# Unused bytes ahead of the activations' buffers: their place relative to the weights' buffers becomes 1216 bytes on by 4096, or 192 by 256

## The chip, the cores and the metric

The kernel runs on one core of a Trainium2 chip. The metric is the device time of one execution in microseconds (us); lower is better. Three executions of the kernel before gave 930.80, 931.08 and 932.78 us, a median of 931.08.

## What is computed

Two layers over 256 tokens of 1024 features, in float32. A layer normalizes its input by the root mean square, makes from it the inputs of four kinds of attention (stick breaking, gated linear, gated delta rule, dilated) and a gate for each, adds up the gated branches and projects them, and then runs an MLP of width 4096 with a squared ReLU:

```
h = rms_norm(x, g_mix)
sb, gla, dn, dil inputs, gate_logits = split(h @ w_in)
o_n = branch n (stick breaking, gated linear attention, delta rule, dilated)
merged = sum over n of sigmoid(gate_logits[n]) * (o_n @ w_branch[n])
x = x + merged @ w_out
h = rms_norm(x, g_mlp)
x = x + square(relu(h @ w_mlp_in)) @ w_mlp_out
```

## The kernel before

**The stream of weights.** All weights are cut into 140 units of 1 MB, 70 to a layer, and each unit into two halves of 512 KB (`raw`, one DMA each). `split_part` (L246 to L248) parts every half into a high part `whi` (ScalarE, L247) and a low part `wlo` (VectorE, L248), both float32r. `split_upto` keeps this three halves ahead of the unit in use (`LEAD`). There are 6 buffers for `raw` and 5 each for `whi` and `wlo`, all of 4096 bytes in a partition.

**The products.** An activation is parted in the same way: `ah` and `al` hold the normalized input, `uh` and `ul` what lies between the two products of the MLP, `oh` and `ol` the output of a branch, `mh0` to `mh3` and `ml0` to `ml3` the merged branches. A float32 product is three float32r products (high by high, high by low, low by high), each with 128 rows, 128 stationary columns and 256 moving columns. A half of a unit is 24 of these. They are all issued by the helper `mm` (L199), and I call them the big products. The small products are those of the branches.

- Feature-major units (`unit_F`: dn_q, dn_k, dn_v, gla_q, sb_q, sb_k, the gates, the first product of the MLP): the weights are stationary, `ah` and `al` move. The output is a bank `bg`.
- Token-major units (`unit_T`: seven in a layer, inT in the list of units): `ah` and `al` are stationary, the weights move.
- The branch products (`unit_br`) move `oh` and `ol`. The projection `wo` and the second product of the MLP are `units_out`: for each half, eight outputs of three products each, with `mh`, `ml` or `uh`, `ul` moving, into banks `fa` and `fb`.

**The order.** It is written out by hand. Per layer: the units of `SEQ` with the four branches, `wo` (4 units), the first product of the MLP (16 units), the second (16 units). The small work of the branches runs in four chains (generators) that go forward by one step at each half of a unit; a table of pauses tells how many halves lie between a step and the one that reads it. All engines work in program order. Early in each mixing part POOL scales x (L369), ScalarE and VectorE rewrite `ah` and `al` from that (`flip`), and TensorE waits for it.

**Where the buffers lie.** Tiles are placed one after the other, in the order in which they are first asked for in their pool: `cons`, `wp` (raw, whi, wlo), `acts` (ah, al), `sm` (small ones), and after these the tiles of the layer's mixing part or of its MLP. Ahead of all lies a scratch region for descriptors of 16384 bytes. With the sizes of the tiles this gives the first byte of each buffer in its partition. What is left of it when multiples of 4096 are taken away:

| buffers | before | distance to the weights by 4096 | by 256 |
|---|---|---|---|
| raw, whi, wlo (all of them) | 2784 | 0 | 0 |
| ah, al | 2784 | 0 | 0 |
| uh, ul | 4000 | 1216 | 192 |
| oh, ol, mh, ml and most of the mixing part | 2240 or 192 (some 1216, 3264) | 3552 or 1504 | 224 |

Inside the buffers the big products step by 512 or 1024 bytes, so that the distance by 256 is the same for every one of a kind.

```
def mm(o, l, r, start=True, stop=True):
    PE.matmul(o, l, r, start=start, stop=stop, skip_group_check=True)
```

In `mm` the second argument is the stationary operand, the third the moving one.

Of the kernel before, what the change touches and what calls it, by code (L numbers as in the profile page):

```python
# [73 lines left out]
# columns of the packed parameters of a layer  # L74
P_GMIX, P_GMLP, P_CONV, P_DTB, P_ALOG, P_GLAB = 0, 8, 16, 40, 44, 48
P_GLAG, P_DNG, P_DILQ, P_DILK, P_LR2, NPAR = 49, 113, 177, 241, 305, 433
# columns of the constants
C_ID, C_NEGU, C_NEG1, C_UT, C_GT, C_STR, C_SBN, C_DIL = 0, 128, 256, 384, 512, 640, 768, 896
C_COS, C_SIN, C_SEL, C_S32, C_I32, C_H4, C_AB, NCON = 1280, 1312, 1344, 1346, 1378, 1410, 1414, 1422
LV = (1, 2, 4, 8, 16, 32, 64)  # L80

# [37 lines left out]
def lay_out(inp):  # L119
    a = {k: np.asarray(v) for k, v in inp.items()}  # L120
    w_in, w_br, w_out, w_mi, w_mo = (a[k] for k in ("w_in", "w_branch", "w_out", "w_mlp_in", "w_mlp_out"))
    W = np.zeros((len(UNITS), 128, 2048), np.float32)

    def kcols(w, c0, n=256):
        """[p][kt][column]"""
        return w[:, c0:c0 + n].reshape(8, 128, n).transpose(1, 0, 2).reshape(128, 8 * n)

    def fcols(w, c0):
        """[p][half of the columns][kt][column]"""
        return w[:, c0:c0 + 256].reshape(8, 128, 2, 128).transpose(1, 2, 0, 3).reshape(128, 2048)  # L130

    def krows(w, r0, halves=1):
        """[p][half of the columns][kt][column]"""
        n = 1024 // halves
        return w[r0:r0 + 256].reshape(2, 128, halves, n).transpose(1, 2, 0, 3).reshape(128, 2048)

    for n, (l, kind, arg) in enumerate(UNITS):
        if kind == "inF":
            W[n] = fcols(w_in[l], OFF[arg])
        elif kind == "inT":  # L140
            W[n] = kcols(w_in[l], OFF[arg])
        elif kind == "mini":
            m = np.zeros((1024, 32), np.float32)
            m[:, 0:8] = w_in[l][:, 2320:2328]
            m[:, 8:24] = w_in[l][:, 1280:1296]
            W[n][:, :256] = kcols(m, 0, 32)
        elif kind == "gate":
            W[n] = fcols(w_in[l], OFF["gates"] + arg[0] * 1024 + arg[1] * 256)
        elif kind == "br":
            W[n] = krows(w_br[l, arg], 0, 2)  # L150
        elif kind == "wo":
            W[n] = krows(w_out[l], arg * 256)
        elif kind == "mi":
            W[n] = fcols(w_mi[l], arg * 256)
        else:
            W[n] = krows(w_mo[l], arg * 256)
    P = np.zeros((NL, 128, NPAR), np.float32)
    for l in range(NL):
        P[l][:, P_GMIX:P_GMIX + 8] = a["norm_mix_g"][l].reshape(8, 128).T
        P[l][:, P_GMLP:P_GMLP + 8] = a["norm_mlp_g"][l].reshape(8, 128).T  # L160
        P[l][:, P_CONV:P_CONV + 24] = a["dn_conv_w"][l].reshape(6, 128, 4).transpose(1, 0, 2).reshape(128, 24)
        P[l][:, P_DTB:P_DTB + 4] = a["dn_dt_bias"][l][None]
        P[l][:, P_ALOG:P_ALOG + 4] = a["dn_a_log"][l][None]
        P[l][:, P_GLAB] = a["gla_b_lr"][l]
        P[l][:, P_GLAG:P_GLAG + 64] = a["gla_norm_g"][l][None]
        P[l][:, P_DNG:P_DNG + 64] = a["dn_norm_g"][l][None]
        P[l][:, P_DILQ:P_DILQ + 64] = a["dil_q_norm_g"][l][None]
        P[l][:, P_DILK:P_DILK + 64] = a["dil_k_norm_g"][l][None]
        for r in (8, 40):
            P[l][r:r + 16, P_LR2:P_LR2 + 128] = a["gla_w_lr2"][l]  # L170
    X = np.ascontiguousarray(a["x"].reshape(256, 8, 128).transpose(2, 1, 0).reshape(128, 2048))
    C, M = constants()
    return {"xin": X, "w": W, "par": P, "con": C, "msk": M}
# [3 lines left out]
def trunk(ctx: ExitStack, tc: tile.TileContext, xin, w, par, con, msk, out, dbg=None, nl=NL):  # L177
# [26 lines left out]
    # ---------------- constants and x  # L204
# [22 lines left out]
    # ---------------- the stream of weights  # L227
# [22 lines left out]
    def split_upto(h):  # L250
        """h counts halves of units"""
        while state["split"] <= min(h, 2 * total - 1):
            k = state["split"]
            hi = wp.tile([128, 1024], F32R, name="whi", bufs=HALVES)
            lo = wp.tile([128, 1024], F32R, name="wlo", bufs=HALVES)
            splits[k] = (hi, lo)
            src = raws.pop(k)
            if wcols(k // 2) == 256:
                # both parts side by side
                src, both = r3(src[:, :128], 4), r3(hi[:, :256], 4)  # L260
                ACT.copy(both[:, :, 0:32], src)
                DVE.tensor_sub(both[:, :, 32:64], src, both[:, :, 0:32].bitcast(F32))
            elif k == 0:
                state["first"] = (src, hi, lo)
            else:
                n = 512 if k == 1 else 1024
                for c in range(0, 1024, n):
                    split_part(src, hi, lo, slice(c, c + n))
            state["split"] += 1
            dma_upto(k + RAW)  # L270
# [20 lines left out]
    # ---------------- small helpers  # L291
    def rsqrt(v, n, name):
        """v: [128, n] in SBUF, > 0"""
        y = sm.tile([128, n], F32, name=name + "y")
        t = sm.tile([128, n], F32, name=name + "t")
        first_guess(v, y, t)
        yield from pause(name)
        newton(v, y, t, POOL if NPOOL else None)
        return y

    def pause(name):
        """slack between a step and the one that reads it on another engine, in halves of units"""
        for _ in range(PAUSE[name]):
            yield
# [15 lines left out]

    def new_act():
        return (acts.tile([128, 8, 256], F32R, name="ah"), acts.tile([128, 8, 256], F32R, name="al"))

    class Norm:
        """x times the gain, feature-major and split; the root mean square is applied to what is made of it"""
# [28 lines left out]
        def rows(self):  # L354
            """1 / rms of each token, on every partition"""
# [9 lines left out]
        def scaled(self, t):  # L365
            """x over the root mean square"""
            self.t = t
            for kt in range(8):
                POOL.tensor_tensor(t[:, kt, :], x[:, kt, :], self.R, op=OP.mult)  # L369

        def flip(self):
            """from here on what is made of it needs no scale"""
# [12 lines left out]
    def half(h, evac_first=False):  # L385
        """weights of half h of the current unit; the halves after it are begun"""
# [11 lines left out]
    def mmF(o, wh, wl, c, h, kts=8, new=False):  # L398
        """feature-major product: three passes; that over the operand split last comes last"""
# [8 lines left out]
    def unit_F(h, new=False):  # L408
        """yields after each half, then a bank [128, 2, 256], feature-major; new: h has only just been made"""
# [7 lines left out]
    def unit_T(h):  # L417
        """token-major, a bank [128, 2, 256]"""
# [12 lines left out]
    def unit_mini(h):  # L431
        """feature-major [64, 256]: by the high parts of the weights and, 32 rows on, by the low ones"""
# [14 lines left out]
    def units_out(h, units, nm):  # L447
        """feature-major products in four banks [128, 2, 256], added to x; the last unit goes by output"""
# [49 lines left out]
    # ---------------- one layer  # L498
# [31 lines left out]
    def mixing(l, pr, mp, nm):  # L530
# [7 lines left out]

        def split_pair(ps):
            pair = [mp.tile([128, 2, 256], F32R, name=n, bufs=2) for n in ("oh", "ol")]  # L540
            split_evac(*pair, ps)
            return pair

        def to_feature(o, br, tag):
            """o: token-major [128, 2, 256] in SBUF -> split feature-major"""
# [7 lines left out]
        def head_rms(o, gs, br, tag, need=None):  # L553
            """o: [128, 2, 4, 64]; gs: silu of the gate times the gain"""
# [16 lines left out]
        # ---- gated delta rule: the gates and their decays  # L571
        def decay_chain():
            yield ("mini",)
            nea = sm.tile([128, 4], F32, name="nea")
# [24 lines left out]
            # rows and columns of the running sums of g  # L599
# [15 lines left out]
            got["E"] = E = T([6, 260], "d6", 3).rearrange("p a b -> p (a b)")[:, :1536].rearrange(  # L615
# [11 lines left out]
        # the products with the queries, and the values  # L627
# [33 lines left out]
        # ---- gated delta rule  # L661
        def dn_chain():
# [4 lines left out]
            pre = T([6, 260], "d6", 3)[:, :, :256]  # L667
# [38 lines left out]
            MT = T([6, 260], "d6", 3).rearrange("p a b -> p (a b)")[:, :1536].rearrange(  # L706
# [23 lines left out]
            # (I + M)^-1 transposed: blocks of 32 by substitution, all heads at once, then by doubling.  # L730
            # mc[j, (t, h), k]: the blocks of -M transposed
# [31 lines left out]
            def half_y(t, s):  # L763
                """levels 32 and 64: only the blocks below the diagonal"""
# [69 lines left out]
        # ---- stick breaking  # L834
# [54 lines left out]
        # ---- dilated  # L889
        def rope_chain():  # L890
            yield ("dil_q", "dil_k")
            qk = got["dil_qk"]                                  # [128, 16 (q/k, t, h), 64]
# [94 lines left out]
        # ---- gated linear attention  # L987
# [41 lines left out]
        def gla_chain():  # L1029
# [24 lines left out]
            # the diagonal and the pairs of level 1, a column of each for a head  # L1054
# [14 lines left out]
            # levels 16 to 2, two at a time; two heads at a time  # L1069
# [31 lines left out]
        # ---- threads of small work beside the weights  # L1101
        done = set()

        class Thread:
# [4 lines left out]
            def advance(self):  # L1109
                """one stage; False when it must wait or is over"""  # L1110
# [53 lines left out]
        cin = T([6, 260], "d6", 3)[:, :, :259]  # L1164
# [129 lines left out]
    with tc.tile_pool(name="boot", bufs=2) as bp:  # L1294
        # the tensor engine is brought to its full clock while the first loads are under way
# [42 lines left out]
```

## Time and profile before

| | |
|---|---|
| median of 3 executions | 931.08 us (930.80 to 932.78) |
| span of the profiled execution | 932.1 us |
| TensorE (PE) busy | 910.4 us, 98% |
| weight loads of TensorE (PEld) busy | 884.4 us, 95% |
| VectorE (DVE) busy | 630.8 us, 68% |
| ScalarE (ACT) busy | 534.4 us, 57% |
| GpSimd (POOL) busy | 143.8 us, 15% |
| read from HBM | 147.51 MB |

The span reaches from the first to the last instruction; it is 1.0 us above the median. Loads of stationary operands overlap the products and are listed apart, as PEld. A product is drawn until its modelled end, 0.28 us after its start, while the next one starts 0.11 to 0.12 us after it: how fast they follow is read from their starts, not from their mean length.

### The profile page before, as it was taken

What the parts mean: (1) busy time and instruction counts of PE and PEld (TensorE: products, weight loads), DVE (VectorE), ACT (ScalarE), POOL (GpSimd) and SP (SyncE); (2) the same over time, 40 slices, a digit from 0 to 9 for tenths busy, and PEclk for the clock granted to TensorE, in tenths of its full rate; (3) what the DMA queues carried; (4) which work ended last, traced back from release to release, by engine and by line L of the source; (5) the groups of instructions that cost most, each with busy time, mean ns of one, the idle gap of its engine ahead of it and who ended that gap; (6) DMA issues with size and microseconds to landing.
All of it is one profiled execution on the core that took longest, in us unless ns stands there. A gap on an engine that the chain in (4) does not pass through costs nothing.

```text
span 932.1 us, 18924 instructions
## 1 busy us (share of the span) xinstructions
PE 910.4 (98%) x7678; PEld 884.4 (95%) x7678; DVE 630.8 (68%) x1242; ACT 534.4 (57%) x842; POOL 143.8 (15%) x148
## 2 busy tenths in 40 slices
PE   8999999999999999999989999999999999999998
PEld 6899999999998999999988999999999989999998
DVE  5959999429577676644489599984485867665442
ACT  5596758754554655543456876586545545654331
POOL 3524201113212000000042450013030120000000
PEclk7999999999999999999999999999999999999999
DMA  8544454433544556656444445444344535656551
GB/s 278 199 139 133 140 178 135 144 130 114 162 142 171 174 190 201 203 188 197 152 135 142 142 132 168 158 138 153 98 154 135 208 113 183 204 197 198 191 161 46
DMA packets 43430, 149.78 MB, mean 161 GB/s; under 512 B 4944, under 2 KB 7248, under 8 KB 43344
## 3 DMA queue, kind: packets, MB, share of 16 engines
q1 hardware_dynamic: 43056, 148.35, 48.8%
q8 instruction: 60, 0.98, 0.4%
q10 hardware_dynamic: 288, 0.23, 0.1%
q14 instruction: 26, 0.21, 0.1%
HBM read 147.51 MB, written 1.05 MB: 159 GB/s over the span
## 4 chain that ended last, share of the span: by engine, by line
PE 84%; DVE 8%; ACT 3%; POOL 2%; issue 1%; DMA 1%; SPq 0%; DVEq 0%; ACTq 0%
PE bg L199 55%; PE fa L199 14%; PE fb L199 14%; POOL s L369 2%; DVE al L339 2%; DVE wlo L248 2%; ACT whi L247 1%; DVE x L486 1%; DMA x<-xin 1%; POOL sbs L859 1%; DVE s L1082 0%; DVE ush L751 0%; DVE ush L749 0%; DVE s L1068 0%; PE fb L972 0%
## 5 line engine op out<-in xcount | busy, mean ns | idle before, releaser
L248 DVE TENSOR_TENSOR wlo<-raw,whi 128x1024 fp32r<-128x1024 f32 (+2 forms) x280 | 350.0, 1268 | 183.0 <-ACT whi L247 182.9
L247 ACT CAST whi<-raw 128x1024 fp32r<-128x1024 f32 (+2 forms) x280 | 283.8, 1034 | 117.9 <-PE bg L199 58.2
L199 PE MATMUL bg<-ah,whi 128*128 128x256 f32 x1232 | 315.2, 292 | 6.4 <-ACT ah L375 4.6
L199 PE MATMUL bg<-al,whi 128*128 128x256 f32 x1232 | 305.6, 289 | 6.2 <-DVE al L339 6.2
L199 PEld LDWEIGHTS bg<-ah,whi 128*128 128x128 f32 x1232 | 239.6, 194 | 13.3 <-ACT ah L375 6.6
L199 PEld LDWEIGHTS bg<-al,whi 128*128 128x128 f32 x1232 | 238.7, 196 | 7.6 <-DVE al L339 7.4
L199 PE MATMUL bg<-ah,wlo 128*128 128x256 f32 x1216 | 179.6, 286 | 1.5 <-DVE wlo L248 1.5
L199 PEld LDWEIGHTS bg<-ah,wlo 128*128 128x128 f32 x1216 | 162.5, 195 | 2.5 <-DVE wlo L248 2.5
L199 PE MATMUL fa<-uh,whi 128*128 128x256 f32 x256 | 70.4, 276 | 0.0
L199 PE MATMUL fa<-uh,wlo 128*128 128x256 f32 x256 | 70.4, 276 | 0.0
L199 PE MATMUL fa<-ul,whi 128*128 128x256 f32 x256 | 69.7, 276 | 0.0
L199 PE MATMUL fb<-uh,whi 128*128 128x256 f32 x224 | 61.6, 276 | 0.0
L199 PE MATMUL fb<-uh,wlo 128*128 128x256 f32 x224 | 61.6, 276 | 0.0
L199 PE MATMUL fb<-ul,whi 128*128 128x256 f32 x224 | 61.0, 276 | 0.0
L513 ACT ACTIVATE sq<-rl 128x512 f32<-128x512 f32 x32 | 20.2, 632 | 70.3 <-DVE rl L512 70.3
L445 DVE TENSOR_TENSOR ul<-sq,uh 128x512 fp32r<-128x512 f32 x32 | 22.2, 693 | 43.2 <-ACT uh L444 43.2
L1271 POOL TENSOR_TENSOR mg<-mg,gt 128x512 f32<-128x512 f32 x20 | 31.1, 1572 | 129.2 <-DVE gt L1270 129.2
L199 PEld LDWEIGHTS fa<-uh,whi 128*128 128x128 f32 x256 | 48.1, 188 | 0.0
L199 PEld LDWEIGHTS fa<-uh,wlo 128*128 128x128 f32 x256 | 48.1, 188 | 0.0
L199 PEld LDWEIGHTS fa<-ul,whi 128*128 128x128 f32 x256 | 47.6, 188 | 0.0
L199 PEld LDWEIGHTS fb<-uh,whi 128*128 128x128 f32 x224 | 42.1, 188 | 0.0
L199 PEld LDWEIGHTS fb<-uh,wlo 128*128 128x128 f32 x224 | 42.0, 188 | 0.0
(276 smaller groups left out, 1470.5 us busy)
## 6 DMA issues: line engine op xcount, KB each, us to landing
raw<-w SPq DMA_DIRECT2D x275, 512.0 KB, 4.3
x<-xin SPq DMA_DIRECT2D x3, 256.0 KB, 6.1
out_dram<-x SPq DMA_DIRECT2D x3, 256.0 KB, 2.1
C<-con SPq DMA_DIRECT2D x1, 519.0 KB, 6.9
raw<-w SPq DMA_DIRECT2D x4, 128.0 KB, 5.3
gt<-msk SPq DMA_DIRECT2D x2, 160.0 KB, 4.7
x<-xin SPq DMA_DIRECT2D x2, 128.0 KB, 2.8
raw<-w SPq DMA_DIRECT2D x4, 64.0 KB, 3.9
```

The lines of the kernel that those rows point to most:

```text
L199: PE.matmul(o, l, r, start=start, stop=stop, skip_group_check=True)
L247: ACT.copy(hi[:, c], src[:, c])
L248: DVE.tensor_sub(lo[:, c], src[:, c], hi[:, c].bitcast(F32))
L339: DVE.scalar_tensor_tensor(self.h[1][:, kt, :], x[:, kt, :], self.g[:, kt:kt + 1], self.h[0][:, kt, :].bitcast(F32), op0=OP.mult, op1=OP.s ...
L369: POOL.tensor_tensor(t[:, kt, :], x[:, kt, :], self.R, op=OP.mult)
L445: DVE.tensor_sub(lo, src, hi.bitcast(F32))
L486: DVE.tensor_add(xs, pairs[fp], xs)
L513: ACT.activation(sq, rl, AF.Square)
L859: POOL.tensor_tensor(sp[:, :, c:c + 128], sp[:, :, c:c + 128], over(STR, 2), op=OP.mult)
L1271: (DVE if n == GLA and MADD[fp] else POOL).tensor_tensor(m, m, g, op=OP.add)
```

## The change

No instruction is added, taken away or moved: on all five queues the same instructions stand in the same order, with the same waits. What changes are places. The scratch region shrinks from 16384 to 4096 bytes, which moves everything by three times 4096. An unused tile of 1216 bytes (`gap`) stands ahead of `ah`. A second one (`gap2`), a wider `nea` and a longer `d6` (1600 instead of 1560 floats, of which the same 1560 are used) set where the later tiles begin.

```
+LATER = 1024 + 192
...
+    acts.tile([128, LATER // 4], F32, name="gap")
+
+    sm.tile([128, 704], F32, name="gap2", bufs=1)
...
+        def d6():
+            return T([1600], "d6", 3)
...
-            nea = sm.tile([128, 4], F32, name="nea")
+            nea = sm.tile([128, 16], F32, name="nea")[:, 0:4]
...
-            got["E"] = E = T([6, 260], "d6", 3).rearrange("p a b -> p (a b)")[:, :1536].rearrange(
+            got["E"] = E = d6()[:, :1536].rearrange(
...
-            pre = T([6, 260], "d6", 3)[:, :, :256]
+            pre = r3(d6()[:, :1560], 6)[:, :, :256]
...
-            MT = T([6, 260], "d6", 3).rearrange("p a b -> p (a b)")[:, :1536].rearrange(
+            MT = d6()[:, :1536].rearrange(
...
-        cin = T([6, 260], "d6", 3)[:, :, :259]
+        cin = r3(d6()[:, :1560], 6)[:, :, :259]
...
-    nc = _bacc.Bacc("TRN2", target_bir_lowering=False, num_devices=1)
+    nc = _bacc.Bacc("TRN2", target_bir_lowering=False, num_devices=1, dynamic_dma_scratch_size=4096)
```

The rest of the diff takes away comments. The places by 4096 become:

| buffers | before | after | distance after, by 4096 | by 256 |
|---|---|---|---|---|
| raw, whi, wlo | 2784 | 2784 | 0 | 0 |
| ah, al | 2784 | 4000 | 1216 | 192 |
| uh, ul | 4000 | 4000 | 1216 | 192 |
| oh, ol, mh, ml | 2240 or 192 (some 1216, 3264) | 2720 or 672 (some 1696, 3744) | 4032, 1984 (some 3008, 960) | 192 |

## Rows read from the trace of the kernel before

**Rows 1.** The page, parts 1 and 4: busy us, share, instructions; chain by engine.

```profile
span 932.1 us, 18924 instructions
...
PE 910.4 (98%) x7678; PEld 884.4 (95%) x7678; DVE 630.8 (68%) x1242; ACT 534.4 (57%) x842; POOL 143.8 (15%) x148
...
PE 84%; DVE 8%; ACT 3%; POOL 2%; issue 1%; DMA 1%; SPq 0%; DVEq 0%; ACTq 0%
```

**Rows 2.** Windows: PE, PEld, DVE, ACT, POOL busy (instructions), clock, DMA share, GB/s.

```profile
300.00:380.00 80.00, 80.00 (x669) 80.00 (x668) 53.99 (x61) 46.92 (x61) 0.00 (x0) 1.00 0.57 185
385.00:463.00 78.00, 78.00 (x690) 78.00 (x690) 36.32 (x31) 31.42 (x30) 0.00 (x0) 1.00 0.58 185
263.20:280.00 16.80, 16.80 (x145) 16.80 (x144) 14.67 (x15) 9.28 (x11) 3.24 (x2) 1.00 0.49 163
```

**Rows 3.** Timeline of PE in three stretches: start, length, what.

```profile
126.80 0.64 PE L199 MATMUL bg<-whi,ah 128*128 128x256 f32 x4
127.28 0.52 PE L199 MATMUL bg<-whi,al 128*128 128x256 f32 x3
...
361.64 1.12 PE L199 MATMUL bg<-ah,wlo 128*128 128x256 f32 x8
362.60 0.28 PE L199 MATMUL bg<-ah,whi 128*128 128x256 f32 x1
...
429.81 0.28 PE L199 MATMUL fa<-ul,whi 128*128 128x256 f32 x1
...
430.61 0.28 PE L199 MATMUL fb<-uh,wlo 128*128 128x256 f32 x1
```

**Rows 4.** Groups of PE: xcount, busy us, mean ns of one, idle before.

```profile
L199 PE MATMUL bg<-ah,whi 128*128 128x256 f32 x1232 | 315.2, 292 | 6.4 <-ACT ah L375 4.6 <-ACT whi L247 1.8
L199 PE MATMUL bg<-al,whi 128*128 128x256 f32 x1232 | 305.6, 289 | 6.2 <-DVE al L339 6.2
L199 PE MATMUL bg<-ah,wlo 128*128 128x256 f32 x1216 | 179.6, 286 | 1.5 <-DVE wlo L248 1.5
...
L199 PE MATMUL bg<-oh,whi 128*128 128x256 f32 x128 | 35.3, 296 | 1.1 <-DVE gt L1270 1.1
...
L199 PE MATMUL bg<-whi,ah 128*128 128x256 f32 x224 | 32.7, 288 | 0.0
...
L199 PE MATMUL fb<-mh,wlo 128*128 128x256 f32 x64 | 17.8, 282 | 0.0
```

**Rows 5.** Span and mean granted clock of the core.

```profile
core 0: 932.1 us, clock 0.983
```

**Rows 6.** Timeline of PE where the clock is at half.

```profile
293.66 0.41 PE L199 MATMUL bg<-al,whi 128*128 128x256 f32 x1
293.87 0.41 PE L199 MATMUL bg<-ah,whi 128*128 128x256 f32 x1
```

**Rows 7.** The chain that ended last, pieces of the first layer: start, length, what.

```profile
23.64 9.15 POOL s L369 x8
...
107.52 1.04 DVE d L649 x4
108.55 1.07 DVE wlo L248
...
111.19 0.66 DVE ol L445
111.90 2.99 PE bg L199 x23
```

**Rows 8.** Windows of two stretches of the mixing part, first layer; columns as above.

```profile
84.00:112.00 28.00, 27.89 (x234) 26.86 (x233) 26.27 (x105) 18.79 (x28) 13.15 (x20) 1.00 0.39 122
...
126.00:163.00 37.00, 37.00 (x308) 36.00 (x307) 35.87 (x164) 28.07 (x55) 3.36 (x4) 1.00 0.45 143
```

**Rows 9.** Groups of DVE: two differences of one shape.

```profile
L445 DVE TENSOR_TENSOR ul<-sq,uh 128x512 fp32r<-128x512 f32 x32 | 22.2, 693 | 43.2 <-ACT uh L444 43.2
...
L1237 DVE TENSOR_TENSOR ml<-mg,mh 128x512 fp32r<-128x512 f32 x8 | 5.3, 686 | 0.4
```

## The prediction, made before the changed kernel was run

> **What bounds the kernel now.** I read the page first. TensorE is busy for 98% of the span and makes up 84% of the chain that ended last; VectorE, the next, has 8% of the chain [rows 1]. So the time is, in the first place, the number of products times the spacing of their starts, and the question is whether that spacing can depend on where the operands lie.
>
> For this I read two stretches in which PE never waits: the first product of the MLP, where `ah` and `al` move, and the second, where `uh` and `ul` move. A product is drawn 0.28 us long and the next starts 0.12 us later, so some 2.4 of each window's count began before it. That gives 80.00 / (669 - 2.4) = 120.0 ns from start to start in the one, and 78.00 / (690 - 2.4) = 113.4 ns in the other [rows 2]. The timeline says the same without a correction: eight products take 362.60 - 361.64 = 0.96 us, 120 ns each; seven take 430.61 - 429.81 = 0.80 us, 114 ns each [rows 3]. The instruction is the same, 128 by 128 stationary and 256 moving float32r columns, and both windows are at the full clock, with DMA at 185 GB/s.
>
> What differs between the two is the place of the operands and the loop around them. The third window of that group tells these apart: `wo` runs in the very loop of the second MLP product, but moves `mh` and `ml`, and takes 16.80 / (145 - 2.4) = 117.8 ns [rows 2]. So one loop has two spacings. By the table of places the three go with the distance by 256: at 0 it is 120.0 ns, at 192 it is 113.4, at 224 it is 117.8. PEld is busy through all of these windows, that is, the load of the next stationary operand goes on beside the present product; the distance of these two reads is what the table is about. I take it that the place is the cause.
>
> [...]
>
> **The change, part by part.** No instruction is added or moved, so each term is a count times a difference of spacing.
>
> (a) Products with `ah` and `al` moving: 1232 + 1232 + 1216 = 3680 [rows 4]. They get the exact places by 4096 that `uh` and `ul` have, against weights that stay where they were, so I use the spacing of those: 120.0 - 113.4 = 6.6 ns, 24.3 us in all. [...] The mean granted clock of 0.983 means 2 x 0.017 x 932.1 = 31.7 us at half, room for 150 products, or 1.0 us [rows 5]. Left: 23.3 us.
>
> (b) Products with `oh`, `ol`, `mh`, `ml` moving: three groups of 128 and six of 64, 768 in all [rows 4]. Their distance by 256 goes from 224 to 192. Their places by 4096 are not those of `uh`, only those by 256; that 256 is the period is not shown beyond the steps of 512 and 1024 inside the buffers, over which each spacing stays the same. I take 117.8 - 113.4 = 4.4 ns, 3.4 us; if they came to 120 instead, it would be a loss of 1.7 us.
>
> (c) Token-major products, three groups of 224, 672 in all [rows 4]: the roles are turned round, and the moving weights now lie 192 behind the stationary activations, where in (a) it is the moving activations that lie 192 on. They take 0.48 us for four today, 120 ns, as in (a) [rows 3]. No row shows this distance. It may go to 113.4 (gain 4.4 us), stay, or go up by one more such step to 126.6 (loss 4.4 us). It is as far from 0 as the good place is, only on the other side; I take half the gain, 2.2 us.
>
> (d) The unused bytes and the smaller scratch cost nothing: nothing fills or reads them. The other engines read and write moved buffers too, but the differences of VectorE on 512 columns take 693 ns at 4000 (`ul`) and 686 at the mixing part's places (`ml`) [rows 9], so a place is worth at most 1% there.
>
> (e) What is given back. A faster TensorE comes sooner to the places where it waits for another engine. A half of a unit is 24 products, so it gains 0.16 us.
> - From 84 to 112 us the chain runs through VectorE, up to the `ol` that TensorE waits for at 111.90 [rows 7]; VectorE is busy for 26.27 of these 28 us [rows 8]. TensorE's gain there, nine halves or 1.4 us, is lost.
> - From 126 to 163 us VectorE is busy for 35.87 of 37.00 us [rows 8]. TensorE would gain 12 halves, 1.9 us, and fall below what VectorE needs. The three halves by which the split weights are ahead cover some of it; I take 0.5 us off.
> - POOL scales x for 9.15 us from 23.64 on, and TensorE waits at its end [rows 7]: the three halves beside it gain nothing, 0.5 us.
> - The other waits are short: in all groups of (a) PE is idle for 6.4 + 6.2 + 1.5 us over both layers, most of it for `al` and `ah` where these are made anew [rows 4]. What the products just before such a wait gain is waited for. I put this at 0.9 us a layer, some six halves.
>
> That is 3.3 us a layer, and the second layer has the same order: 6.6 us.
>
> Sum: 23.3 + 3.4 + 2.2 - 6.6 = 22.3 us. The profiled span of 932.1 becomes 909.8; the median of the runs is 1.0 below the span, so I predict 908.8 us.
>
> What is late next, where TensorE is no longer: in the mixing part VectorE, with 97% of the stretch from 126 to 163 us. In the MLP the stream of weights must deliver 512 KB in 24 x 113.4 = 2.72 us; it does so already through the second MLP product, at 185 GB/s [rows 2].
>
> **The rivals.**
>
> 1. Place does nothing, and the spacing belongs to something else in these stretches. For it: one loop takes one activation for eight outputs, the other takes a new one for every two or three products. Against it: `wo`, with 117.8 ns in the loop that has 113.4 elsewhere. Time: 931.
>
> 2. The mixing parts give everything back, because VectorE, or the steps that go to and fro between the engines, set their pace. Then only the MLP and `wo` gain: 2 x (768 x 6.6 + 192 x 4.4) ns = 11.8 us, so 919.3. For it: two stretches, 65 us of a layer, with VectorE at 94 and 97% [rows 8]. Against it: PE was busy for 27.89 and all of 37.00 us of them and VectorE's share of the whole chain is 8% [rows 1].
>
> 3. Slower: the distance that is good in the loop of eight outputs is bad in the feature-major loop, where weights and activation step together. One more step up, to 126.6 ns, over 3680 products is 24 us, so 955; it turns into a loss as soon as these products average over 120.0. Against it: the distance by 256 is the same for every step of both loops, and at distance 0 each step of the feature-major and of the token-major loop takes the same 120.
>
> **How the numbers follow.** I give the forecast 84%, rival 1 4%, rival 2 9% and rival 3 2%; 1% is left for a gain beyond all the terms. Within the forecast, the upper end takes twice what is given back and nothing from (c): 931.1 - (23.3 + 3.4 - 13.2) = 917.6. The lower end takes (c) in full and nothing given back: 931.1 - (23.3 + 3.4 + 4.4) = 900.0. A stretch of half clock more or less, 3.4 us long as a rule, moves either end by some 1.5 us. I give 899 to 918, which leaves out rivals 1 to 3. About 0.2%, 1.9 us, is what a measurement of this kernel can tell from no change: faster 0.94, same 0.04, slower 0.02.
>
> **What would show each step right or wrong.** In the first MLP product a half must take 2.72 instead of 2.88 us, and a window of 80 us there must count some 38 products more; if it does not, (a) is wrong and all falls. The timeline of `wo` at 113 to 114 ns shows (b). The groups `bg<-whi,ah` show (c), either way. For (e): the wait for `ol` near 110 us should grow by 1 us or more, and new waits of PE for VectorE should appear in the mixing parts, 5 to 8 us in all; more than 13 us of them would make the prediction wrong on the slow side.

## The result and the profile after

Four executions of the changed kernel gave 917.39 (the profiled one), 920.86, 916.94 and 924.88 us, a median of 919.12; beside them the kernel before gave 930.80 to 935.84, median 931.93. The ratio is 0.9859, 95% interval 0.9830 to 0.9887. The change makes the kernel faster, as forecast, but by 12.8 us where 22.3 were forecast, and 919.12 lies 1.1 us above the range.

The page of the kernel after, its first lines and its chain by engine (what answers to [rows 1]), and its mean granted clock ([rows 5]):

```profile
span 915.6 us, 18924 instructions
...
PE 891.4 (97%) x7678; PEld 864.9 (94%) x7678; DVE 629.2 (69%) x1242; ACT 534.0 (58%) x842; POOL 141.8 (15%) x148
...
PE 80%; DVE 11%; ACT 4%; POOL 3%; issue 1%; DMA 1%; SPq 0%; DVEq 0%; ACTq 0%
```

```profile
core 0: 915.6 us, clock 0.979
```

TensorE is still the bound; its busy time fell by 19.0 us, and VectorE has 11% of the chain instead of 8%. The next view is windows of the kernel after, columns as in [rows 2]: the first and the second MLP product of the first layer, and the two stretches of the mixing part that [rows 8] show.

```profile
300.00:365.00 65.00, 65.00 (x575) 65.00 (x575) 45.38 (x51) 38.42 (x49) 0.00 (x0) 1.00 0.59 190
385.00:450.00 65.00, 65.00 (x575) 65.00 (x575) 29.14 (x25) 25.33 (x24) 0.00 (x0) 1.00 0.62 197
...
84.00:112.00 28.00, 27.09 (x233) 26.07 (x232) 26.27 (x102) 19.64 (x29) 13.31 (x20) 1.00 0.38 121
126.00:163.00 37.00, 37.00 (x328) 35.84 (x328) 34.93 (x156) 29.71 (x56) 3.61 (x4) 1.00 0.49 155
```

The first MLP product went from 120.0 to 65.00 / (575 - 2.4) = 113.5 ns, as the second had before. In 84 to 112 us TensorE does no more than before (233 products against 234) and idles 0.8 us more. In 126 to 163 us it does 20 more, with no idle time.

Groups of PE in the kernel after, for [rows 4]:

```profile
L203 PE MATMUL bg<-ah,whi 128*128 128x256 f32 x1232 | 305.4, 288 | 6.0 <-ACT ah L383 3.9
L203 PE MATMUL bg<-al,whi 128*128 128x256 f32 x1232 | 294.8, 284 | 6.2 <-DVE al L347 6.2
...
L203 PE MATMUL bg<-ah,wlo 128*128 128x256 f32 x1216 | 173.5, 281 | 1.5 <-DVE wlo L252 1.5
...
L203 PE MATMUL bg<-whi,ah 128*128 128x256 f32 x224 | 32.2, 285 | 0.0
```

The idle time before the first three hardly changed (6.4, 6.2 and 1.5 us before), and the token-major products of the fourth, the roles turned round, are 3 ns shorter as drawn. The wait for `ol` did grow. The timeline of PE where [rows 7] show TensorE at 111.90, the kernel before and then the kernel after:

```profile
111.51 0.28 PE L199 MATMUL bg<-oh,whi 128*128 128x256 f32 x1
111.90 0.39 PE L199 MATMUL bg<-ol,whi 128*128 128x256 f32 x1
```

```profile
108.03 1.11 PE L203 MATMUL bg<-ah,wlo 128*128 128x256 f32 x8
108.97 0.28 PE L203 MATMUL bg<-oh,whi 128*128 128x256 f32 x1
110.16 0.38 PE L203 MATMUL bg<-ol,whi 128*128 128x256 f32 x1 [0.91 <-DVE ol L453]
```

From the start of the one product to that of the other it is 0.39 us before and 1.19 after, 0.80 more. The view of the kernel after also shows what the forecast had not reckoned with: eight products with `ah` take 108.97 - 108.03 = 0.94 us, 117.5 ns each, not 113.4.

### The profile page after: what moved, and what is told of

It reads as the page before. It is cut to its first block, busy times and chain, and to the rows that moved or that the text cites. A ratio compares the mean times of both kernels' runs of the same rounds, so it can differ in the third digit from the quotient of the medians.

```text
span 915.6 us, 18924 instructions
## 1 busy us (share of the span) xinstructions
PE 891.4 (97%) x7678; PEld 864.9 (94%) x7678; DVE 629.2 (69%) x1242; ACT 534.0 (58%) x842; POOL 141.8 (15%) x148
## 4 chain that ended last, share of the span: by engine, by line
PE 80%; DVE 11%; ACT 4%; POOL 3%; issue 1%; DMA 1%; SPq 0%; DVEq 0%; ACTq 0%
PE bg L203 51%; PE fb L203 14%; PE fa L203 14%; DVE wlo L252 3%; POOL s L377 2%; DVE al L347 2%; ACT whi L251 1%; POOL sbs L870 1%; DVE x L494 1%; DMA raw<-w 1%; DVE ush L762 1%; DVE ush L760 1%; DVE Y L764 1%; DVE s L1093 1%; DVE d L650 0%
## 5 line engine op out<-in xcount | busy, mean ns | idle before, releaser
L203 PE MATMUL bg<-ah,whi 128*128 128x256 f32 x1232 | 305.4, 288 | 6.0 <-ACT ah L383 3.9
L203 PE MATMUL bg<-al,whi 128*128 128x256 f32 x1232 | 294.8, 284 | 6.2 <-DVE al L347 6.2
L203 PEld LDWEIGHTS bg<-ah,whi 128*128 128x128 f32 x1232 | 236.7, 192 | 13.7 <-ACT ah L383 6.2
L203 PEld LDWEIGHTS bg<-al,whi 128*128 128x128 f32 x1232 | 235.5, 194 | 7.6 <-DVE al L347 7.4
L203 PE MATMUL bg<-ah,wlo 128*128 128x256 f32 x1216 | 173.5, 281 | 1.5 <-DVE wlo L252 1.5
L203 PEld LDWEIGHTS bg<-ah,wlo 128*128 128x128 f32 x1216 | 156.3, 191 | 2.4 <-DVE wlo L252 2.4
```

## The experiments

I took the spacing from the starts of the big products: the mean of all gaps up to 126 ns, over each part of the program. "Above 113.33" in the first table is the sum of what these gaps have above 113.33 ns, in us of the profiled execution. "MLP 1" and "MLP 2" are the first and the second MLP product, first and second layer, in ns, read in 65 us of each. A trace is of one execution, which need not be near the median: that of d128 took 933.92 us (median 926.69), that of e_more 912.58 (median 917.70).

| kernel | place of `ah`, `al` by 256 | MLP 1 | MLP 2 | above 113.33 |
|---|---|---|---|---|
| before | 0 | 120.0, 120.0 | 113.4, 113.4 | 29.8 |
| after | 192 | 113.4, 113.4 | 113.3, 113.3 | 7.6 |
| a_again (the same) | 192 | 117.8, 113.4 | 117.8, 113.3 | 15.0 |
| p192 | 192 | 113.4, 117.7 | 113.3, 117.8 | 13.8 |
| d0_mix_only | 0 | 119.9, 119.9 | 113.4, 113.4 | 27.1 |
| d64 | 64 | 117.8, 117.8 | 117.8, 117.8 | 23.4 |
| d96 | 96 | 120.0, 120.0 | 113.4, 113.4 | 26.7 |
| d128 | 128 | 118.7, 118.7 | 117.8, 113.3 | 27.5 |
| d160 | 160 | 118.7, 117.4 | 117.8, 117.8 | 28.4 |
| d224 | 224 | 118.3, 118.3 | 113.3, 113.3 | 21.0 |
| e_fast | 192 | 113.4, 113.4 | 113.4, 113.4 | 7.4 |
| e_slow | 192 | 117.8, 117.8 | 117.8, 113.4 | 17.3 |
| e_more | 192 | 113.4, 113.4 | 113.4, 113.4 | 6.9 |
| acts_only | 192 | 113.4, 113.4 | 113.4, 113.4 | 8.5 |

**a_again: the changed kernel once more, without an edit.**

> The changed kernel once more, nothing altered. Theory A (more than one settled spacing): at distance 192 the products settle either at 113.4 or near 118 ns, and which one is chosen anew at the start of each unbroken run of products. Then another execution shows the same halves of units at other durations: some of the 2.83 us halves of the gates come at 2.72 us and some of the 2.72 us ones at 2.83 us, and the time differs between executions by several us, with the count of products near 118. Theory B (other engines): the 118 ns stretches come from what the other engines do beside them. Then the same halves are at 2.83 us again, all others at 2.72, and the times lie within 2 us but for the half-clock stretches.

Measured: 920.33 us (915.80 to 923.15), ratio 0.9857 (0.9815 to 0.9900). Windows of this execution, the two MLP products of each layer:

```profile
300.00:365.00 65.00, 65.00 (x554) 65.00 (x553) 45.46 (x50) 38.02 (x49) 0.00 (x0) 1.00 0.57 190
385.00:450.00 65.00, 65.00 (x554) 65.00 (x553) 28.17 (x24) 24.22 (x23) 0.00 (x0) 1.00 0.57 187
760.00:825.00 65.00, 65.00 (x576) 65.00 (x575) 44.55 (x49) 39.66 (x52) 0.00 (x0) 1.00 0.60 199
845.00:910.00 65.00, 65.00 (x576) 65.00 (x575) 27.67 (x23) 23.21 (x22) 0.00 (x0) 1.00 0.44 148
```

The program, its places and the full clock are the same. Yet a whole MLP part, both products, went at 65.00 / (554 - 2.4) = 117.8 ns in the first layer and at 113.3 in the second. So the place alone doesn't set the spacing: at distance 192 there are two, and these four stages each kept one. The choice fell before the stage. TensorE just ahead of the first MLP product, first layer, in the same execution:

```profile
285.56 0.39 PE L203 MATMUL bg<-al,whi 128*128 128x256 f32 x1 [1.04 <-DVE al L347]
286.97 0.39 PE L203 MATMUL bg<-al,whi 128*128 128x256 f32 x1 [1.03 <-DVE al L347]
...
290.02 0.28 PE L203 MATMUL bg<-ah,whi 128*128 128x256 f32 x1
...
291.90 1.10 PE L203 MATMUL bg<-ah,wlo 128*128 128x256 f32 x8
292.84 0.59 PE L203 MATMUL bg<-nsum,C 128*128 128x256 f32 x2
...
293.39 0.28 PE L203 MATMUL bg<-al,whi 128*128 128x256 f32 x1
...
294.10 0.28 PE L203 MATMUL bg<-al,whi 128*128 128x256 f32 x1
```

Sixteen products from 290.02 us on, ahead of the small one for the norm (`bg<-nsum,C`) take 1.88 us, 117.5 ns each, and six behind it 0.71, 118.3 each. In all twelve such places of after, a_again, p192 and the three kernels with an added product below, the spacing ahead of it (8 short, 4 long) was the one behind it.

**The distance, one at a time.** All these keep the later tiles and `uh`, `ul` where the changed kernel has them, and move `ah` and `al` alone. For d128:

```
-LATER = 1024 + 192
+LATER = 1152
...
-    sm.tile([128, 704], F32, name="gap2", bufs=1)
+    sm.tile([128, 720], F32, name="gap2", bufs=1)
```

The others have 1024 + 0, 64, 96, 160 and 224 in the first line and `gap2` changed by as many bytes the other way; p192 has 192 and 960, so that the distance is 192 by 256 and by 4096.

> ah and al go back to distance 0 by 256 (1024 by 4096); the mixing part's tiles and all else stay as in the changed kernel. If the distance by 256 is what counts, the products with ah and al are at 120.0 ns again in the first MLP product (a half takes 2.88 us), although their place by 4096 is 1024 away from that of before, and the time is that of before less at most 3 us, 928 to 932. If the place by 4096 counts, they do not go to 120.0 and the time stays near 918.

> ah and al at 192 by 4096 instead of 1216: the same distance by 256, another by 512, 1024 and 4096. If the period is 256, the first MLP product takes 2.72 us a half (or 2.83 where it settles at the other spacing) and the time is that of the changed kernel, 917 to 925. If the longer distance counts, the spacing is another one, and the time too.

> ah and al at distance 128 by 256 (1152 by 4096), half way round; nothing else moved. Theory A: the spacing belongs to the distance between the read of the moving operand and that of the next stationary one, so it has a value of its own here, the same for both roles (128 either way round): feature-major and token-major products at one spacing. It should be clear of 120.0; no row tells whether below or above 113.4. A view in which only 0 is bad and everything else is good says 113.4 for both, and a time of 905 to 918.

> ah and al at distance 64 by 256 (1088 by 4096), the mirror image of 192; nothing else moved. If the spacing hangs on the distance between the two reads whichever way round, feature-major products take the two spacings that token-major ones show at 192, 113.4 and 117.8 ns, in runs of products, and the time is 915 to 925. If the side counts, the first MLP product shows another spacing.

> ah and al at distance 96 by 256. Between 64 (expected 113.4 or 117.8) and 128 (118.8 measured as a mean): if the spacing changes step by step with the distance, a mean of 113 to 119 ns in the first MLP product; time 914 to 928. What it is to tell: whether a distance has only the low spacing.

> ah and al at distance 160 by 256, between 128 (mean 118.8, never settled) and 192 (113.4 or 117.8). A view in which farther from 0 is better says 113.4 or below; the measured 118.8 at 128 speaks against that, and by it 160 is 115 to 119 ns. Time 914 to 928.

> ah and al at distance 224 by 256, which the mixing part's tiles had before the change, where products came at 115 to 123 ns, a mean of 118.3, never settled. The same for ah and al: a mean of 117.5 to 118.5 ns in the first MLP product, a half at 2.84 us, and a time of 922 to 929. If the place of the mixing tiles and not the distance made those 118.3, it is something else.

Measured: d0_mix_only 931.55 us, ratio 0.9987 (0.9969 to 1.0004); p192 918.63, 0.9852 (0.9816 to 0.9888); d64 924.20, 0.9920 (0.9884 to 0.9957); d96 928.50, 0.9959 (0.9931 to 0.9988); d128 926.69, 0.9939 (0.9913 to 0.9965); d160 932.11, 0.9993 (0.9963 to 1.0023); d224 926.73, 0.9937 (0.9891 to 0.9984). The first MLP product in windows of p192 (both layers), then one window each of d0_mix_only, d64, d128 and d224:

```profile
300.00:365.00 65.00, 65.00 (x576) 65.00 (x575) 44.38 (x49) 39.79 (x51) 0.00 (x0) 1.00 0.59 194
760.00:825.00 65.00, 65.00 (x554) 65.00 (x553) 45.41 (x51) 39.24 (x50) 0.00 (x0) 1.00 0.61 202
```

```profile
300.00:365.00 65.00, 65.00 (x544) 65.00 (x543) 43.90 (x49) 39.38 (x51) 0.00 (x0) 1.00 0.59 195
```

```profile
300.00:365.00 65.00, 65.00 (x554) 65.00 (x553) 44.75 (x50) 38.70 (x50) 0.00 (x0) 1.00 0.59 193
```

```profile
300.00:365.00 65.00, 65.00 (x550) 65.00 (x550) 45.22 (x51) 37.66 (x49) 0.00 (x0) 1.00 0.56 183
```

```profile
300.00:365.00 65.00, 65.00 (x552) 65.00 (x551) 44.05 (x50) 39.65 (x51) 0.00 (x0) 1.00 0.58 194
```

Counts of 576, 554, 544, 550 and 552 are 113.3, 117.8, 120.0, 118.7 and 118.3 ns. Moving `ah` and `al` back to 0 takes most of the gain away, so most of it is theirs. The rest, 1.2 us by the ratio and within its interval of nothing, shows at equal clocks (see the last table below): 931.08 to 931.68 us at 0.983, where the kernel before takes 933.07 to 934.42, and 929.87 and 929.97 at 0.985, where it takes 931.22 to 931.93. That is some 2 us for the mixing tiles' shift, whose products came at 114.1 (`unit_br`) and 114.3 ns (`wo`) there instead of 118.2 and 118.3.

p192 keeps the whole gain (918.63 us, 113.4 and 117.7 ns), so a move by 1024 bytes changed nothing that these runs show. That the period is as short as 256 rests on the mixing tiles. After the change they lie 448 on by 512, which is 192 by 256, and their products take the two spacings that `ah` has at 192 by 512 (113.3 and 117.8 ns in `wo` of the kernel after); before it they lay 480 on, which is 224 by 256, with a mean of 118.3 ns, as `ah` has in d224 at 224 by 512. Of the distances tried, 192 alone gave whole stages of the first product at 113.4.

d0_mix_only, p192, d64 and d224 came inside the times expected; d96 (to 928) and d160 (to 928) were slower. 96, between 64 and 128, is back at 120.0, so the spacing doesn't change step by step with the distance. d128 has one spacing for both roles, as expected: 118.7 ns feature-major and 118.6 token-major. d64 sat at 117.8 in all four MLP stages, two of which move `uh` and `ul`, untouched and at 192: the 113.4 of [rows 2] is not fixed for them either.

**What chooses between the two.** One guess was the work of the other engines. Against it, windows and starts of products in the kernel after:

```profile
90.80:95.90 5.10, 5.10 (x47) 5.10 (x47) 5.10 (x27) 4.64 (x9) 5.10 (x10) 1.00 0.38 106
237.50:245.50 8.00, 8.00 (x71) 8.00 (x70) 4.07 (x8) 4.11 (x8) 0.12 (x1) 1.00 0.44 133
```

```profile
90.39 0.40 PE L203 MATMUL fb<-sp,NR 128*128 128x256 f32 x2
90.63 0.28 PE L203 MATMUL bg<-ah,whi 128*128 128x256 f32 x1
...
93.35 0.28 PE L203 MATMUL bg<-ah,whi 128*128 128x256 f32 x1
...
240.07 0.28 PE L203 MATMUL bg<-ah,whi 128*128 128x256 f32 x1
...
242.90 0.28 PE L203 MATMUL bg<-ah,whi 128*128 128x256 f32 x1
```

With VectorE and POOL busy all the time, a half of 24 products takes 93.35 - 90.63 = 2.72 us, the short spacing; with VectorE half idle and POOL idle it takes 2.83, the long one. What many of the runs of products at one spacing had in common was the small product just ahead of them. Over six traces (after, a_again, p192, e_fast, e_slow, e_more; names are output<-moving, stationary), `fb<-sp,NR` ahead of `ah`, seen at 90.39 above, was followed by the short spacing 12 times in 12, `fa<-T,d`, with 32 stationary columns, 24 times in 24, while `fb<-sb_k,s` and `fa<-Vs,U` were followed by the long one 12 times in 12 each. Some are mixed (`fa<-d`: 3 short, 9 long), and it isn't the small product alone: ahead of token-major products the same `fb<-sp,NR` was followed by the long spacing 9 times in 12.

**e_fast and e_slow: a small product more, ahead of a run.** Its output is read by nobody; it is added ahead of the third unit of the first MLP product and ahead of the second MLP product, in both layers. e_fast adds one with 32 stationary columns, e_slow one with 128 and 64 moving columns:

```
+    def breaker():
+        ps = bank("fa")
+        mm(ps[96:128, 0:32], C[64:96, 96:128], C[64:96, 0:32])
...
+                if g == 2:
+                    breaker()
                 for n, ps in enumerate(unit_F(nm.h, g == 0)):
...
+            breaker()
             units_out(lambda kt: (uh[:, kt, :], ul[:, kt, :]), 16, nm)
```

```
+        mm(ps[:, 0:64], ID, C[:, 0:64])
```

> One product of 32 rows, 32 stationary and 32 moving columns in float32, whose output nobody reads, is added ahead of unit 2 of the first MLP product and ahead of the second one, four in all. Theory A: at distance 192 the spacing of a whole run of products is set by how it starts, that is by the product just ahead of it; in three executions runs behind such a 32-column product of the branches came at 113.4 in 22 of 24 cases. Then all four MLP stages are at 113.4 ns in the profile (a half at 2.72 us), the executions differ less, and the median falls to 913 to 917, for a cost of some 0.25 us a product. The rival, that a stage is low or high by chance in each execution whatever stands ahead of it: two of the six (layer, execution) pairs of the changed kernel ran at 117.8, so a stage at 117.8 in this profile or a median of 918 to 921 is for the rival.

> The same places, but the added product has 128 rows, 128 stationary and 64 moving columns; behind products of that kind in the branches runs came at 117.8 in 12 of 12 cases. Theory A: all four MLP stages are at 117.8 (a half at 2.83 us), 3000 products by 4.4 ns or 13 us more than where they are all at 113.4: a median of 926 to 931. The rival: no different from the other kernel with an added product, 917 to 922.

Measured: e_fast 920.36 us (916.50 to 920.87), ratio 0.9869 (0.9847 to 0.9891); e_slow 923.52 (920.97 to 925.71), 0.9911 (0.9888 to 0.9933). The timeline of PE in e_fast around the added product (`fa<-C`), second layer:

```profile
747.21 0.28 PE L203 MATMUL bg<-ah,whi 128*128 128x256 f32 x1
...
748.62 1.10 PE L203 MATMUL bg<-ah,wlo 128*128 128x256 f32 x8
749.66 0.24 PE L203 MATMUL fa<-C 32*32 32x32 f32 x2
...
750.29 0.28 PE L203 MATMUL bg<-al,whi 128*128 128x256 f32 x1
...
751.76 0.50 PE L203 MATMUL bg<-ah,wlo 128*128 128x256 f32 x3
```

Twelve products ahead of it take 1.41 us, 117.5 ns each; thirteen behind it 1.47, 113.1 each. In e_slow, first layer, it goes the other way:

```profile
294.36 0.28 PE L203 MATMUL bg<-al,whi 128*128 128x256 f32 x1
...
295.83 1.07 PE L203 MATMUL bg<-ah,wlo 128*128 128x256 f32 x8
296.74 0.33 PE L203 MATMUL fa<-C 128*128 128x64 f32 x2
...
297.08 0.28 PE L203 MATMUL bg<-al,whi 128*128 128x256 f32 x1
...
298.73 0.28 PE L203 MATMUL bg<-al,whi 128*128 128x256 f32 x1
```

Thirteen take 1.47 us, 113.1 ns each, ahead of it; fourteen 1.65, 117.9 each, behind it. Same operands, same place, same loop: a product between switched the spacing, and three whole stages followed (window of e_slow, second layer, first product, then second):

```profile
760.00:825.00 65.00, 65.00 (x554) 65.00 (x554) 45.45 (x50) 37.91 (x49) 0.00 (x0) 1.00 0.61 198
845.00:910.00 65.00, 65.00 (x576) 65.00 (x575) 27.89 (x23) 23.21 (x22) 0.00 (x0) 1.00 0.44 144
```

The fourth didn't: there the products had the long spacing ahead of the same added product and 113.3 behind it. Of the eight places the spacing changed in three, once to short in e_fast and once each way in e_slow; in the others it already was what it became. So the 64-column product does not force the long spacing, and with four places its leaning to it is thinly shown. Both times missed. For e_fast 913 to 917 was expected: its spacings were right in all stages behind the added product, but it ran at a low clock, 0.978 to 0.979 in four of five executions, and at 0.979 it took 918.91 to 920.40 where the changed kernel took 917.39 (last table), so no gain over that kernel is shown. For e_slow 926 to 931 was expected, with all four stages long. At one clock the two kernels are far apart, 925.71 us for e_slow at 0.983 and 916.50 for e_fast, one execution each; their traces differ by 9.9 us above 113.33.

**e_more: the 32-column product at more places.** Also ahead of `wo`, after the transposes of `Gc` and after the products into `pd`, ten added products in all instead of four:

```
+            breaker()
             units_out(lambda kt: (m[kt // 2][0][:, kt % 2, :], m[kt // 2][1][:, kt % 2, :]), 4, nm)
...
+            breaker(pc)
             yield from pause("e10")
...
+            breaker(pb)
             yield from pause("g13")
```

> The 32-column product also ahead of the projection wo and behind the transposes of the running sums and the diagonal products of gated linear attention, where long runs (70, 118 and 128 products) came at 117.8: ten added products in all. Theory A: 0.3 to 0.5 us a run less, minus 0.1 to 0.25 us for the product itself, so 0.5 to 1.5 us less than with four; a median of 912 to 917. The rival: the added products cost 2 us and give nothing.

Measured: 917.70 us (912.58 to 920.48), ratio 0.9838 (0.9811 to 0.9864). The median lies just above the 912 to 917 expected. The MLP stages were all at 113.4, and what is above 113.33 fell to 6.9 us, 0.5 less than in e_fast; but at one clock e_more is no faster than e_fast (last table), so that the added places pay isn't shown. Its `wo` also left the short spacing in both layers with no product between and no gap over 122 ns. First layer:

```profile
264.31 0.28 PE L203 MATMUL fb<-ml,whi 128*128 128x256 f32 x1
...
265.44 0.28 PE L203 MATMUL fb<-mh,wlo 128*128 128x256 f32 x1
...
266.14 0.28 PE L203 MATMUL fa<-mh,wlo 128*128 128x256 f32 x1
...
267.79 0.28 PE L203 MATMUL fb<-ml,whi 128*128 128x256 f32 x1
```

Ten products take 1.13 us, 113 ns each, and soon after fourteen take 1.65, 117.9 each. So a run mostly keeps its spacing, but not always.

**acts_only: the mixing tiles back at 224.** Only the unused floats of `d6` are taken out, so that `oh`, `ol`, `mh`, `ml` and the small tiles stand by 256 as in the kernel before.

```
         def d6():
-            return T([1600], "d6", 3)
+            return T([1560], "d6", 3)
```

> The changed kernel with the mixing part's tiles back at their places of before (2240 and 192 by 4096, distance 224); ah and al stay at distance 192. Term (b) alone is undone. Theory A: branch products and wo at 118.3 ns as a mean, never settled, instead of 113.4 or 117.8; 768 products by 2.7 to 4.4 ns, 2 to 3.4 us more product time than in the changed kernel, all else alike, the MLP and the gates at 113.4 or 117.8 by runs. A median of 919 to 924. If the shift of the mixing tiles also matters to the other engines, the time moves by more than that.

Measured: 917.45 us (912.29 to 921.02), ratio 0.9835 (0.9796 to 0.9874). It was expected to lose and didn't. `wo` and the branch products went back to 118.3 and 118.1 ns, as before the change, but the gates, with `ah` and `al` moving, fell from 115.8 and 115.4 to 114.3 and 114.5. Four small products that had the long spacing behind them every time in the six traces, `sb_k,s`, `Vs,U`, `C,dlT` and `sba,sb_v`, now had the short one, twice each, while `sp,NR` ahead of `ah` had the long one once in two. So the kind of small product doesn't decide by itself; that the place of its operands counts is one reading, from one trace. Term (b) is real (d0_mix_only has it alone), but undoing it cost no time that these executions show: 1474 gate products at some 1.2 ns less are 1.8 us, near the 2.3 us of (b). That the shift of the mixing tiles is what lengthened the gates isn't shown.

**Time at one clock.** In the kernel before, time follows the mean granted clock of the execution, from a median of 930.5 us at 0.989 to one of 936.0 at 0.980. 62 executions of it, run beside these experiments, tell what it takes at each clock; the table sets executions of the others beside it, in us. Clocks with few executions are left out.

| clock | before, median | after, a_again | p192 | e_fast | e_more | acts_only |
|---|---|---|---|---|---|---|
| 0.989 | 930.5 (7, 929.8 to 930.7) | 916.94, 924.88 | | | 912.58, 912.83 | |
| 0.987 | 930.9 (12, 929.9 to 931.2) | | | | | 912.29 |
| 0.985 | 931.7 (9, 931.2 to 931.9) | 920.86 | | | | 914.20, 919.56, 920.28, 921.02 |
| 0.983 | 933.6 (11, 933.1 to 934.4) | 922.15 | 920.38, 915.27 | 916.50 | 917.57, 917.83, 918.26 | 915.33 |
| 0.981 | | 915.80, 923.15 | 916.88, 921.95 | | | |
| 0.980 | 936.0 (15, 935.0 to 936.9) | 918.50 | | | | |
| 0.979 | | 917.39 | | 918.91, 920.36, 920.40 | 920.48 | |

At one clock the kernel before agrees within 2 us, e_fast within 1.5 and e_more within 0.7, but the changed kernel's two executions at 0.989 lie 7.9 us apart, a_again's at 0.981 7.4, and acts_only's at 0.985 6.8. The choice of spacing would do that: one layer's whole MLP part, 1536 products, costs 6.8 us more at 117.8 than at 113.4. The traces, one for each kernel, show it directly only for the profiled execution (a_again, 15.0 us above 113.33 and 922.15 us; after, 7.6 and 917.39).

## Why the prediction was wrong in size and right in sign

**That the place of the operands matters (the root of all terms): right.** d0_mix_only undoes it for `ah` and `al` alone and loses all but some 2 us of the gain. Rival 1 falls: 120.0, 118.7 and 113.4 ns for one instruction at three distances. That no place matters does not hold here; whether PE's two reads hold each other up, or another engine's accesses do, no run here shows.

**Term (a), 23.3 us, is the step that failed.** It took "the spacing of those", the 113.4 ns of `uh` and `ul`, for the one spacing of distance 192. That was one of two. [rows 2] showed it in one long unbroken run, 690 products, and such a run mostly keeps one spacing. In the profile after, the products with `ah` or `al` moving came to a mean of 114.55 ns, from 119.75, over the 3,430 gaps at full clock: 17.9 us. (32 of the 3680 products have 64 stationary columns, which makes 0.2 us of the term.) Terms (b) and (c) rest on the same number: (b) gave 118.25 to 115.1 over 730, 2.3 us for 3.4; (c) 119.8 to 117.0 over 640, 1.8 us for 2.2, so the turned roles gain too. In all 22.0 us for 28.9 there; in a_again 29.8 - 15.0 = 14.8, in p192 16.0. The range's upper end took nothing from (c) but kept (a) and (b) in full, so it had no room for this.

**Term (e), 6.6 us given back, was over-sized in the profiled execution.** The waits of PE that have a name went from 18.2 to 20.4 us, 2.2 more. The first bullet came as said: in 84 to 112 us nothing was gained, and the wait for `ol` grew by 0.80 us, a little less than the 1 us asked for. The second did not: TensorE gained 20 products in 126 to 163 us, where VectorE had been busy for 97%, and VectorE itself fell to 34.93 us.

**The clock stood in the range alone, with 1.5 us.** In the profiled execution it was 0.979, not 0.983. [rows 5] give 31.7 us at half clock, in which the starts of [rows 6], 0.21 us apart, make the 150 products of term (a); here it is 2 x 0.021 x 915.6 = 38.5 us. Those 6.8 us more hold 32 products at 0.21 us where they would hold 60 at 0.1134, so some 28 products, 3.1 us, are lost. Against the span: 22.0 - 2.2 - 3.1 = 16.7, and it fell by 932.1 - 915.6 = 16.5. These three account for the profiled span, which lies 5.8 us above the 909.8 forecast.

**The step from span to median failed too.** The other 4.5 of the 10.3 us by which 919.12 lies above 908.8 are there: the prediction took the median to lie 1.0 us below the profiled span, and it lies 3.5 above it. Every execution after lies 1.7 to 1.9 us above its own span, so the 1.0 only told that the profiled execution before was slower than the median. The profiled one after was the second fastest of four, at the lowest clock; 924.88 us at 0.989 can't be laid to the clock. That such executions had the long spacing in a stage, as a_again did, is inferred from the table at one clock, and no trace of them shows it.

**Rival 2 has the right time, 919.3, by luck.** By it the mixing parts give all back and the MLP gains in full. In fact the normalized-input products of the mixing part came down too (feature-major units 119.6 to 114.6 ns, gates 119.7 to 115.6). Rival 3, a step up to 126.6, was seen at none of the distances tried.

**What stays open.** Why one small product leads to the short spacing and another to the long one. The added products of e_fast (32 by 32 columns) and e_slow (128 by 64) differ in stationary and in moving columns at once, and that in acts_only the same small products at other places had the other spacing behind them is from one trace, so which of the three counts isn't told apart. In e_slow's last stage 113.3 ns followed the same product that had led to 117.9 elsewhere, so the product alone doesn't settle it. The norm's small product left the spacing as it was 12 times in 12, and `wo` of e_more went from 113 to 117.9 ns with no product between. In the profile after, five half-clock stretches ended among big products (next starts at 16.03, 36.51, 289.02, 487.03 and 743.10 us), and behind each of them these settled at 113 to 114 ns. e_more and acts_only have lower medians than the change, but their intervals overlap its 0.983 to 0.9887; that either beats it isn't shown.

## What to carry to other kernels

Where TensorE is the bound, compare the spacing of equal products in different stages: if it differs with the operands' place by 256 bytes (113.4 to 120.0 ns here), unused bytes ahead of a buffer are worth trying, and the sweep must be run, since six of the seven distances tried here gave less. A spacing read in one stage of one execution is a sample; read it in every layer and in a second execution before it is multiplied by thousands of products. Compare single executions only at the same mean clock.

## What was not expected of the hardware

- One instruction with one pair of places has two settled spacings, 113.4 and 117.8 ns, each kept over windows of 550 products and more. A single small product added between switched it to 113.4 once in e_fast, and once each way in e_slow.
- By distance the first MLP product took 120.0 ns at 0, 117.8 at 64, 120.0 at 96, 118.7 at 128, 117.4 to 118.7 at 160, 113.4 or 117.8 at 192, 118.3 at 224.
- The mean clock of an execution is worth as much as the change's own spread: e_more took 912.58 us at 0.989 and 920.48 at 0.979. In the kernel after, one half-clock stretch (granted clock 0.50, starts 0.21 us apart from 286.46 us on) came behind two idle times of 1.04 and 1.03 us, in which TensorE waited for `al`. In a_again the same two idle times ended at 285.56 and 286.97 us (lines above), and the products behind them went on at full clock, 117.5 ns apart.
